# A small first load ahead of the 14-row loads in a row-sum kernel

## The chip, the cores and the metric

One core of one Trainium2 chip. The metric is the device time of one execution in microseconds (us); the profiles' spans are some 1.6 us shorter than that time and are used to say where it goes. All runs quoted are of one core.

## The reference

```python
def setup_inputs():
    batch, seq, dim = 32, 512, 1024
    return {"x": np.random.randn(batch, seq, dim).astype(np.float32), "divisor": float(dim)}

def reference(x, divisor):
    return (np.sum(x, axis=-1) / divisor).astype(np.float32)
```

16,384 rows of 1,024 float32 (67.1 MB) are read once from HBM, the chip's main memory; 64 KB are written. Each of 128 partitions has 128 rows of 4 KB to sum.

## The kernel before

All loads are issued by the SyncEngine's queue (SP), in order. Rows 0 to 119 of each partition (the main part) come in loads of 14 rows, then 8; the number beside each is how many of its rows the ScalarE (ACT) sums, while VectorE (DVE) sums the others in one instruction. The last 8 rows per partition come in ever smaller loads, so that little is left to sum when the last byte lands. Three tiles of 14 rows rotate: the fourth load waits until the first tile is summed. The first three loads wait for nothing and are put ahead of the start-up barrier.

```python
def start_loads_at_once(nc):
    first, body = nc.main_func.blocks[0], nc.main_func.blocks[1]
    loads = []
    for i in body.instructions:
        if i.engine == SP:
            if type(i).__name__ != "InstDMACopy" or (i.sync_info and i.sync_info.on_wait):
                break
            loads.append(i)
    names = {i.name for i in loads}
    ...  # moved from the body into the first block
...
    L = 8
    M = J - L                      # 120
    ...
    main = [(14, 0)] * 6 + [(14, 4), (14, 6), (8, 4)]
    last = [(4, 2), (2, 1)]
    assert sum(n for n, _ in main) == M and sum(n for n, _ in last) == L - 2
    bulk = ctx.enter_context(tc.tile_pool(name="bulk", bufs=3))
    ...
    def sums(dst, t, rows, on_act):
        d = rows - on_act
        for i in range(d, rows):
            act_sum(dst[:, i : i + 1], t[:, i, :])
        nc.vector.reduce_sum(out=dst[:, :d], in_=t[:, :d, :], axis=AX)

    j = 0
    for rows, on_act in main:
        t = bulk.tile([P, 14, D], F32, name="t")
        load(t[:, :rows, :], x_main[:, j : j + rows, :])
        sums(res[:, j : j + rows], t, rows, on_act)
        j += rows
    ...  # then loads of 4, 2 and 1 rows, and the last row in three pieces: pa, pb, pc
```

The rows of one load lie together both in HBM and in the tile, so a load is one packet per partition: 56 KB for 14 rows, 8 KB for 2. A DMA engine serves 8 partitions, 8 packets per load.

## Time and profile before

| | before |
|---|---|
| time, median of 4 runs | 161.69 us (161.69 to 161.78) |
| span of the profile | 160.1 us |
| share of the 16 DMA engines | 97.8% |
| DVE busy | 119.9 us |
| landing of the first load | 19.56 us |
| DVE's last work starts | 158.18 us |

The profile is read by the arrivals. An engine that only follows the DMA starts each instruction about 0.02 us after a load has landed, so the start times of DVE's sums in the timeline are a clock for the DMA stream. The time between two such starts for full 14-row loads is called the beat below. The prediction below shows these lines. The sum that ends the kernel, also from the timeline (start, duration, engine, line, operation):

```profile
158.18 0.49 DVE L195 TENSOR_SCALAR_CACHE_REDUCE scaled<-pc 128x322 f32<-128x322 f32 x1
```

It waits for the last piece of the last row. Whatever moves this line moves the time.

### The profile page before, as it was taken

Reading aid. Unit: us, or ns where it says so; the run is one execution under the profiler, and the core shown is the slowest. Engines: PE = TensorE matmul, PEld = TensorE weight load, DVE = VectorE, ACT = ScalarE, POOL = GpSimd, SP = SyncE. Lnnn points to the kernel's source line nnn. Section 1 sums busy time; section 2 is a strip of 40 time slices with the busy share of each in tenths; the row PEclk is TensorE's granted clock in tenths of the full one; section 3 lists DMA queues with packets and bytes.
Section 4 is the critical chain, followed back from the end, with each engine's and each line's share of the span. In section 5 each row is a group of like instructions: output and inputs, shape, how many; then the busy total and the mean of one; then the engine's idle time right before and its main releaser. Section 6 shows DMA issues by size and latency. Waiting matters only on the chain.

```text
span 160.1 us, 138 instructions
## 1 busy us (share of the span) xinstructions
DVE 119.9 (75%) x16; ACT 20.7 (13%) x39; POOL 0.8 (1%) x6
## 2 busy tenths in 40 slices
DVE  0000199968998699959995999599987990497985
ACT  3000000000000000000000000000007300491973
POOL 0000000000000000000000000000000000000010
DMA  8899999998899999998899999999799999999993
GB/s 301 387 458 458 458 458 458 458 430 358 358 458 458 458 458 458 458 458 387 358 401 458 458 458 458 458 458 430 315 401 458 458 458 458 393 393 405 415 402 104
DMA packets 2448, 67.18 MB, mean 419 GB/s; under 512 B 528, under 2 KB 912, under 8 KB 1040
## 3 DMA queue, kind: packets, MB, share of 16 engines
q1 hardware_dynamic: 2448, 67.18, 97.8%
HBM read 67.11 MB, written 0.07 MB: 419 GB/s over the span
## 4 chain that ended last, share of the span: by engine, by line
DMA 67%; DVE 29%; another core or an unknown queue 1%; SPq 1%; issue 0%; DVEq 0%
DMA t<-in_x_dram 45%; DVE res L153 28%; DMA row<-in_x_dram 22%; SPq L142 1%; DVE q L173 1%; DVE scaled L195 0%; DVE pc L190 0%; DVE fin L191 0%; DVEq L195 0%; DVEq L229 0%
## 5 line engine op out<-in xcount | busy, mean ns | idle before, releaser
L153 DVE TENSOR_REDUCE res<-t 128x14 f32<-128x14336 f32 (+3 forms) x9 | 114.4, 12716 | 37.9 <-DMA t<-in_x_dram 37.9
L147 ACT ACTIVATE junk<-t 128x1024 f32<-128x1024 f32 x17 | 17.2, 1011 | 135.2 <-DMA t<-in_x_dram 135.2
L153 DVE TENSOR_REDUCE q<-t 128x2 f32<-128x2048 f32 (+1 forms) x2 | 3.5, 1752 | 0.7 <-DMA t<-in_x_dram 0.7
L147 ACT ACTIVATION_READ_ACCUMULATOR junk<-t 128x1 f32 x17 | 3.2, 186 | 0.0
L147 ACT ACT_TABLE_LOAD x1 | 1.3, 1283 | 1.7 <-PEq L215 1.7
L186 POOL TENSOR_SCALAR res<-res 128x120 f32<-128x120 f32 x1 | 0.5, 512 | 150.5 <-DVE res L153 150.5
L173 DVE TENSOR_REDUCE q<-row 128x1 f32<-128x768 f32 x1 | 1.0, 953 | 0.1
L195 DVE TENSOR_SCALAR_CACHE_REDUCE scaled<-pc 128x322 f32<-128x322 f32 x1 | 0.5, 490 | 0.1
L147 ACT ACTIVATE junk<-pa 128x448 f32<-128x448 f32 x1 | 0.5, 547 | 0.1
L190 DVE TENSOR_REDUCE pc<-pb 128x1 f32<-128x256 f32 x1 | 0.4, 412 | 0.0
L147 ACT ACTIVATE junk<-row 128x256 f32<-128x256 f32 x1 | 0.4, 387 | 0.1
L191 DVE SCALAR_TENSOR_TENSOR fin<-q,r 128x7 f32<-128x7 f32 x1 | 0.2, 167 | 0.0
L147 ACT ACTIVATION_READ_ACCUMULATOR junk<-row 128x1 f32 x1 | 0.2, 187 | 0.0
L147 ACT ACTIVATION_READ_ACCUMULATOR junk<-pa 128x1 f32 x1 | 0.2, 186 | 0.0
L139 POOL MEMSET r<- 128x8 f32 x1 | 0.1, 104 | 1.3 <-POOLq L215 1.3
L215 POOL MEMSET const-bfloat16-1.0<- 128x1 bf16 x1 | 0.1, 101 | 0.0
L215 POOL MEMSET const-uint8-127<- 128x1 uint8 x1 | 0.1, 101 | 0.0
L215 POOL MEMSET const-float32-0.0<- 128x1 f32 x1 | 0.1, 99 | 0.2 <-issue 0.2
L215 POOL MEMSET const-float32-1.0<- 128x1 f32 x1 | 0.1, 98 | 0.0
L195 DVE DVE_READ_ACCUMULATOR scaled<-pc 128x1 f32 x1 | 0.1, 82 | 0.0
## 6 DMA issues: line engine op xcount, KB each, us to landing
t<-in_x_dram SPq DMA_DIRECT2D x8, 7168.0 KB, 35.7
t<-in_x_dram SPq DMA_DIRECT2D x1, 4096.0 KB, 28.5
t<-in_x_dram SPq DMA_DIRECT2D x1, 2048.0 KB, 33.0
t<-in_x_dram SPq DMA_DIRECT2D x1, 1024.0 KB, 35.0
row<-in_x_dram SPq DMA_DIRECT2D x1, 512.0 KB, 35.8
pa<-in_x_dram SPq DMA_DIRECT2D x1, 224.0 KB, 36.0
pc<-in_x_dram SPq DMA_DIRECT2D x1, 160.0 KB, 35.7
pb<-in_x_dram SPq DMA_DIRECT2D x1, 128.0 KB, 35.9
```

Source lines behind the costliest of these rows:

```text
L139: nc.gpsimd.memset(r, 0.0)
L142: tc.keep_in_program_order(nc.sync.dma_start(out=dst, in_=src))
L147: nc.scalar.activation(junk[:, :n], src, COPY, scale=by, accum_out=dst)
L153: nc.vector.reduce_sum(out=dst[:, :d], in_=t[:, :d, :], axis=AX)
L173: nc.vector.reduce_sum(out=q[:, j : j + 1], in_=row[:, :c], axis=AX)
L186: nc.gpsimd.tensor_scalar_mul(out=res, in0=res, scalar1=scale)
L190: nc.vector.reduce_sum(out=pc[:, D - b + 1 :], in_=pb, axis=AX)
L191: nc.vector.scalar_tensor_tensor(out=fin[:, : L - 1], in0=q[:, : L - 1], scalar=scale, in1=r[:, : L - 1], op0=MULT, op1=ADD)
L195: nc.vector.tensor_scalar(out=scaled, in0=pc, scalar1=scale, scalar2=0.0, op0=MULT, op1=ADD, accum_out=fin[:, L - 1 :])
L215: nc = _bacc.Bacc("TRN2", target_bir_lowering=False, num_devices=1)
```

## The change

Its intent: start with a load of 2 rows, whose packets are 8 KB, and take the two rows off a later load, which becomes 12.

```diff
-    main = [(14, 0)] * 6 + [(14, 4), (14, 6), (8, 4)]
+    main = [(2, 0)] + [(14, 0)] * 6 + [(14, 4), (12, 5), (8, 4)]
```

## The prediction

> **What bounds the kernel now.** I read the page first (busy shares, then the DMA lines), then the timeline for the arrival of each load, then the rate by stretches, then the DMA queue's own waits, and last the first 20 us of the DMA alone.
>
> The page, busy shares, DMA line by slices, and the queue:
>
> ```profile
> DVE 119.9 (75%) x16; ACT 20.7 (13%) x39; POOL 0.8 (1%) x6
> ...
> DMA  8899999998899999998899999999799999999993
> ...
> DMA packets 2448, 67.18 MB, mean 419 GB/s; under 512 B 528, under 2 KB 912, under 8 KB 1040
> ...
> q1 hardware_dynamic: 2448, 67.18, 97.8%
> ```
>
> The 16 DMA engines are busy for 97.8% of 160.1 us; the next busiest thing, DVE, has 25% to spare. The slices marked 7 or 8 in the middle are not holes: these views book a packet at its start, and packets here last some 2 us, so slices alternate (later ones read more than 100%). The timeline, DVE lines only, in us from the start: start, duration, and in brackets the idle time before:
>
> ```profile
> 19.58 15.09 DVE L153 TENSOR_REDUCE res<-t 128x14 f32<-128x14336 f32 x1 [19.58 <-DMA t<-in_x_dram]
> 36.52 15.09 DVE L153 TENSOR_REDUCE res<-t 128x14 f32<-128x14336 f32 x1 [1.86 <-DMA t<-in_x_dram]
> 53.47 15.09 DVE L153 TENSOR_REDUCE res<-t 128x14 f32<-128x14336 f32 x1 [1.86 <-DMA t<-in_x_dram]
> ...
> 138.18 8.69 DVE L153 TENSOR_REDUCE res<-t 128x8 f32<-128x8192 f32 x1 [6.13 <-DMA t<-in_x_dram]
> ...
> 147.89 4.42 DVE L153 TENSOR_REDUCE res<-t 128x4 f32<-128x4096 f32 x1 [1.02 <-DMA t<-in_x_dram]
> ...
> 152.79 2.29 DVE L153 TENSOR_REDUCE q<-t 128x2 f32<-128x2048 f32 x1 [0.48 <-DMA t<-in_x_dram]
> ...
> 155.29 1.22 DVE L153 TENSOR_REDUCE q<-t 128x1 f32<-128x1024 f32 x1 [0.21 <-DMA t<-in_x_dram]
> ```
>
> Every reduce of a load starts when that load lands, and DVE idles 0.2 to 6 us before it. Full loads land 16.94 to 16.95 us apart, whatever DVE does. The rate by stretches of one or two such beats (start:end, length, DVE, ACT, POOL, clock, DMA share, GB/s):
>
> ```profile
> 36.40:53.40 17.00, 15.09 (x1) 0.00 (x0) 0.00 (x0) 1.00 1.00 432
> 53.40:87.30 33.90, 30.17 (x2) 0.00 (x0) 0.00 (x0) 1.00 1.00 433
> 87.30:121.10 33.80, 30.17 (x2) 0.00 (x0) 0.00 (x0) 1.00 1.00 434
> ```
>
> The DMA share is 1.00 and the rate flat at 432 to 434 GB/s. So the time is one uninterrupted stream of 67.1 MB, plus what precedes its first byte, plus a short end. Linking packet records engine by engine, I find no pause above 0.05 us on any of the 16 engines between the first packet and the end of the loads.
>
> The DMA queue's own waits (us in total, times, longest):
>
> ```profile
> SPq L142 <- DVE res L153: 90.5, 6, 15.1
> SPq L142 <- DMA t<-in_x_dram: 25.3, 6, 17.9
> ```
>
> They look large, but they only hold back issues that are early anyway: the fourth load is issued when reduce 0 ends at 34.67, while the third load lands at 53.45, so 18.8 us of work is still queued.
>
> **What the Trainium skill says.** "DMA: Bandwidth & Descriptors", section Where 436 GB/s comes from, gives 435.2 GB/s as the limit of the 16 SBUF ports; the trace's 433 agrees within 0.5%, so there is no rate left to win. The same page, Anatomy of one DMA, gives about 2 us of fixed cost for a DMA, mostly completion, fitted on the other (GpSimd) issue path; in this queue, where the next load is already waiting, a load costs only about 0.09 us of its own (worked out below), so the fixed part shows only at the start and the end. "Perfetto Trace Analysis", section DMA Optimizations, says that splitting DMAs may let work start sooner where the DMA engines are generally idle; here they are not. The first page's Why small descriptors are slow names a fixed overhead of about 3 cycles per packet, which falls with packet size: 3 beats in 256 for 8 KB against 3 in 1792 for 56 KB, 1% of a load of 2.4 us, an estimate of 0.03 us; the trace has more, see below, and the trace decides.
>
> **The change part by part.**
>
> 1. Rows and loads. Before, the main loads are 14 x 8, then 8 rows (120); after, 2, then 14 x 7, 12, 8 (120). Same bytes, one load more, and 128 more data packets (2 rows are one 8 KB packet per partition, 8 packets per DMA engine). What a load costs beyond its bytes comes from the landings above: 14 rows take 16.945 us; 2 rows take 155.29 - 152.79 = 2.50. Slope (16.945 - 2.50)/12 = 1.204 us per row, fixed part 2.50 - 2.41 = 0.09 us. Test: 8 rows give 9.72 (measured 147.89 - 138.18 = 9.71), 4 rows 4.91 (152.79 - 147.89 = 4.90). So one more load costs 0.09 us on the path that sets the end.
>
> 2. Start. The first load landed at 19.58; less 16.945 that is a start of 2.64 us: issue, descriptor generation, the slow first packets, completion. If it stays, the landings after are: 2.64 + 2.50 = 5.14 for the 2 rows, then 22.1, 39.0, 56.0, 72.9, 89.9, 106.8, 123.75 for the fourteens, 138.3 for the twelve (14.54 us), 148.0 for the eight. Everything from there to the end is the same sequence, about 0.1 us later than before.
>
> 3. The early reduce. A reduce of 2 rows, 2.29 us, is added at 5.1, where DVE only waited before. On the late side the 12-row load gives DVE 7 rows and ACT 5 in place of 8 and 6: DVE 7.6 us (1.067 per row from 15.09 and 2.29, plus 0.15) against 8.69, ACT one row (1.01 + 0.19 us) less. DVE busy should read about 121.1, ACT about 19.5. All of it is beside the stream: after the twelve lands at 138.3, DVE is done at 145.9 and idles until 148.0. None of the gain of the earlier first reduce reaches the end, because DVE has 1.86 us of slack in every 16.95 and has nothing to catch up.
>
> 4. Buffers. Three buffers before and after, but the first now holds 2 rows. Its reduce ends at 7.4, so load 3 is issued at 7.4 rather than waiting until 34.7. Load 4 is issued at 22.1 + 15.1 = 37.2, when load 3 has until 56.0 to run; each later one 18.8 us ahead of need; the eight is issued at 121.9, 16.4 ahead. The stream is never short.
>
> 5. Semaphores. The order of instructions shows that one more load moves the rotation of DMA semaphores by one: the last small load (pc) now waits for the last fourteen (123.75) and not for the one before it (121.2). It is issued some 1.6 us later, 33 us before it lands. The early output store waits for the twelve (138.3), long before its data. No cost.
>
> 6. Slow first packets. By the packet records, each DMA engine's first 56 KB packet takes 2.25 to 3.35 us, mean about 2.9, where all later ones take 2.12; the starts are spread from 1.02 to 1.83 us and the ends from 3.85 to 4.38. The slices of the first 20 us (half a us each) show the same waves:
>
> ```profile
> DMA  0096000990029000950099009900790009500990
> GB/s 0 0 1606 229 0 0 0 573 1262 0 0 115 1720 0 0 0 1606 229 0 0 1147 688 0 0 459 1376 0 0 344 1491 0 0 0 1606 229 0 0 1376 459 0
> ```
>
> The first wave of starts falls in the third and fourth slices, the second only in the eighth and ninth. This loss of about 0.8 us per engine is the one thing on the path that the first load's shape can alter. If it is a fixed delay of the first access, it stays whatever the packet size. If it is a slower rate over the whole first packet, small packets may shorten it, and with eight of them the engines may spread less than the 0.53 us they carry to the end.
>
> Sum: +0.09 for the load, 0 for DVE, ACT, buffers and semaphores, and for the start 0 to -0.7; I take a quarter chance or so of most of it, -0.2. 161.7 + 0.09 - 0.2 = 161.6 us.
>
> **The rivals.**
>
> - The intent, a gain by early work: DVE starts at 5.1 in place of 19.6, 14.4 us sooner, and if DVE set the end the time would drop towards 150. Against it: DVE idles before every reduce for a landing. It would make nothing.
> - A shorter start: the slow first packets shrink with their size. For it, the excess in the first packet only; against it, late starters lose least (the one at 1.83 us took 2.25), which looks like a common moment before which nothing flows, about 1.7 to 2.2 us, independent of size. It would give 161.0 to 161.3.
> - A hole after the small load: it lasts 2.5 us, so the second load's descriptors must be there by about 4 us. The queue's first instructions take 0.33 to 0.43 us each and the first packet began 1.02 us after its issue, so the second load could start at about 1.5. Were there a hole, it would be 0.5 to 1 us: 162.3 to 162.8.
> - A late buffer: if issues came too late the fourteen-row beat would break; with 16 us in hand I give it almost nothing.
>
> **Range and chances.** Two per cent is 3.2 us. The start, all of it, is 2.64 us, and at most 0.8 of that is open to the change; the sure cost is 0.09. Nothing I can find reaches 2% either way. The three runs before lie within 0.1 us. The range of 161.0 to 162.0 holds the full gain at the start and a small loss there. Chances: faster 0.01, within 0.98, slower 0.01.
>
> **What would show each step right or wrong.** Right: a reduce of 2 rows at about 5.1 us; fourteens landing 16.95 apart from 22.1; the eight at 148.0; stretches still at 1.00 and 433 GB/s; DVE busy 121.1; span 160.0 to 160.3. If the small load lands well before 4.6 or the second before 21.6, the start got shorter (step 6). If the second lands after 22.5, there is a hole or the 8 KB packets are dearer than 0.09 in all (steps 1 and 2). If the beat of 16.95 changes, the address pattern matters to the rate, and my sum is void. If the first landings shift and the end does not, something behind the loads, not the stream, sets the end.

## The result, and the profile after

| | before | after |
|---|---|---|
| time, median of 4 runs | 161.69 us (161.69 to 161.78) | 161.44 us (161.41 to 161.48) |
| span | 160.1 us | 159.9 us |
| DVE busy | 119.9 us | 121.1 us |
| ACT busy | 20.7 us | 19.7 us |

The ratio is 0.9983, with a 95% interval of 0.9966 to 1.0000. Ratios here are the mean time of one kernel's fast runs over that of the other's of the same rounds, so not quite the ratio of the medians. In absolute terms 0.25 us are gone. The interval reaches 1, so this pair alone does not yet show a gain; the experiments below have to.

The page of the changed kernel, busy shares and DMA queue:

```profile
DVE 121.1 (76%) x17; ACT 19.7 (12%) x37; POOL 0.8 (1%) x6
...
q1 hardware_dynamic: 2592, 67.18, 97.9%
```

Still one DMA stream, with 144 packets more. The timeline of the changed kernel, DVE only:

```profile
4.83 2.29 DVE L153 TENSOR_REDUCE res<-t 128x2 f32<-128x2048 f32 x1 [4.83 <-DMA t<-in_x_dram]
21.76 15.09 DVE L153 TENSOR_REDUCE res<-t 128x14 f32<-128x14336 f32 x1 [14.65 <-DMA t<-in_x_dram]
38.70 15.09 DVE L153 TENSOR_REDUCE res<-t 128x14 f32<-128x14336 f32 x1 [1.85 <-DMA t<-in_x_dram]
...
137.94 7.62 DVE L153 TENSOR_REDUCE res<-t 128x7 f32<-128x7168 f32 x1 [3.72 <-DMA t<-in_x_dram]
...
147.66 4.42 DVE L153 TENSOR_REDUCE res<-t 128x4 f32<-128x4096 f32 x1 [2.09 <-DMA t<-in_x_dram]
...
157.93 0.49 DVE L195 TENSOR_SCALAR_CACHE_REDUCE scaled<-pc 128x322 f32<-128x322 f32 x1
```

DVE is at work at 4.83 in place of 19.58, and then idles 14.65 us for the next landing: the early start is given straight back. The 14-row beat is the same, 38.70 - 21.76 = 16.94. By the rates by stretches it is the same stream too:

```profile
22.00:38.90 16.90, 15.04 (x2) 0.00 (x0) 0.00 (x0) 1.00 1.00 434
38.90:72.80 33.90, 30.18 (x3) 0.00 (x0) 0.00 (x0) 1.00 1.00 433
```

The difference is at the beginning. Before, DVE began the first 14 rows at 19.58; at 16.945 us for a full load that is a start of 2.63 us. After, it began the first 2 rows at 4.83; at the 2.50 us that a 2-row load takes within the stream, a start of 2.33. So the stream started 0.30 us sooner. The load of 8 rows is then 0.23 sooner (147.66 against 147.89) and the last sum 0.25 (157.93 against 158.18): by this reckoning 0.05 to 0.07 us of the start are spent on the load added. These two numbers are the whole result.

The queue's waits are as harmless as before; there is one more of each kind:

```profile
SPq L142 <- DVE res L153: 92.8, 7, 15.1
SPq L142 <- DMA t<-in_x_dram: 24.8, 7, 14.3
```

### The profile page after: what moved, and what is told of

Read it like the earlier page. It is cut to its first block, busy times and chain, and to the rows that moved or that the text cites. A ratio compares the mean times of both kernels' runs of the same rounds, so it can differ in the third digit from the quotient of the medians.

```text
span 159.9 us, 139 instructions
## 1 busy us (share of the span) xinstructions
DVE 121.1 (76%) x17; ACT 19.7 (12%) x37; POOL 0.8 (1%) x6
## 4 chain that ended last, share of the span: by engine, by line
DMA 77%; DVE 22%; SPq 1%; issue 0%; DVEq 0%
DMA t<-in_x_dram 56%; DMA row<-in_x_dram 21%; DVE res L153 20%; SPq L142 1%; DVE q L173 1%; DVE scaled L195 0%; DVE pc L190 0%; DVE fin L191 0%; DVEq L195 0%; DVEq L229 0%
## 5 line engine op out<-in xcount | busy, mean ns | idle before, releaser
L153 DVE TENSOR_REDUCE res<-t 128x14 f32<-128x14336 f32 (+4 forms) x10 | 115.7, 11566 | 36.4 <-DMA t<-in_x_dram 36.4
L147 ACT ACTIVATE junk<-t 128x1024 f32<-128x1024 f32 x16 | 16.2, 1014 | 136.0 <-DMA t<-in_x_dram 136.0
```

The lines of the kernel that those rows point to most:

```text
L147: nc.scalar.activation(junk[:, :n], src, COPY, scale=by, accum_out=dst)
```

## The experiments

The sizes at stake are 0.1 to 0.3 us, and a chip's runs of the same kernel can scatter by as much, so each experiment is read twice: by the ratio of times, and by the start of the stream in its profile. The start is the time at which DVE begins its first sum, less what the first load takes within the stream (0.0925 + 1.204 us per row, from the prediction's step 1). The kernels of a call share a chip and the runs of the kernel before.

| kernel | first load, packets | DVE starts | start of the stream | last sum starts | median, before | ratio (95%) |
|---|---|---|---|---|---|---|
| before | 14 rows, 56 KB | 19.58 | 2.63 | 158.18 | | |
| before_again | 14 rows, 56 KB | 19.48 | 2.53 | 158.05 | 161.82, 161.74 | 1.0005 (0.9992 to 1.0017) |
| second2 | 14 rows, 56 KB | 19.38 | 2.43 | 158.02 | 161.91, 161.80 | 1.0001 (0.9986 to 1.0016) |
| early1_14 | 14 rows, 56 KB | 19.64 | 2.69 | 158.23 | 161.80, 161.74 | 1.0008 (0.9996 to 1.0021) |
| pad2 | 14 rows, 56 KB | 19.70 | 2.75 | 158.32 | 161.78, 161.71 | 1.0003 (0.9991 to 1.0015) |
| pad0 | 14 rows, 8 KB | 20.07 | 2.75 | 158.31 | 161.84, 161.71 | 1.0008 (0.9995 to 1.0021) |
| first7 | 7 rows, 28 KB | 11.02 | 2.50 | 158.09 | 161.56, 161.80 | 0.9983 (0.9970 to 0.9995) |
| first4 | 4 rows, 16 KB | 7.28 | 2.37 | 157.99 | 161.62, 161.80 | 0.9984 (0.9971 to 0.9996) |
| after | 2 rows, 8 KB | 4.83 | 2.33 | 157.93 | 161.44, 161.69 | 0.9983 (0.9966 to 1.0000) |
| after_again | 2 rows, 8 KB | 4.85 | 2.35 | 158.69 | 161.54, 161.71 | 0.9994 (0.9979 to 1.0009) |
| near2 | 2 rows, 8 KB | 4.83 | 2.33 | 157.93 | 161.52, 161.71 | 0.9992 (0.9980 to 1.0004) |
| early1_2 | 2 rows, 8 KB | 4.78 | 2.28 | 157.86 | 161.38, 161.74 | 0.9983 (0.9970 to 0.9997) |
| half2 | 2 rows, 4 KB | 4.86 | 2.30 | 157.99 | 161.65, 161.74 | 0.9992 (0.9980 to 1.0005) |
| first1 | 1 row, 4 KB | 4.01 | 2.71 | 158.28 | 161.59, 161.80 | 0.9982 (0.9969 to 0.9995) |

For pad0 its own load time is taken off, 17.32 us, and for half2 0.06 more than for 2 rows (8 packets of 7 ns). The start column is one execution each. Over the five kernels that begin with 14 rows in 56 KB packets it is 2.61 in the mean (2.43 to 2.75), over the four with 2 rows in 8 KB packets 2.32 (2.28 to 2.35): 0.29 us, and the two ranges don't touch.

The ranges are those of the profiled runs, and a profile can fall on a good run of its kernel or a bad one: second2's fell on its fastest (161.55, median 161.91), first1's on its slowest. In twelve of the fourteen profiles the time of the profiled run is its start plus 159.04 to 159.14 us (half2 159.21, after_again 159.86, see there). So, in the profiles, what makes one run slower than another is mostly its start, and single starts of the two kinds of kernel can overlap; the means differ.

From the start to the last sum it is 155.52 to 155.55 in before, before_again and early1_14, and 155.57 to 155.62 in seven kernels with one load more (second2, first1, first4, first7, after, near2, early1_2). So the load added costs about 0.05 us, whether it stands first or second. (Half2 has more packets besides, and after_again was held up on the way.)

The packet records give a second reading of the start, which needs neither DVE nor the landing: when each of the 16 DMA engines ends its share of the first load, less what these packets take later in the stream. The mean of the 16 engines is 1.90 to 2.03 us in the five kernels with 14 rows in 56 KB packets, 1.91 in pad0, 1.88 with 7 rows, 1.75 with 4, 1.66 to 1.73 in the five with 2 rows, and 1.86 in first1. The engines end about as far apart as before (0.52 us between the first and the last in the kernel before, 0.49 in the changed one). By this measure the first engine moved from 1.72 to 1.42 and the last from 2.24 to 1.91: both by about 0.3.

The theories at the outset. **A:** the very first packets are slow, and lose less when they are small; what the change gains is there. **B:** the gain comes from the later part, the 14, 12, 8 split or the shifted rotation.

### The same loads with the small one second (second2)

```diff
-    main = [(2, 0)] + [(14, 0)] * 6 + [(14, 4), (12, 5), (8, 4)]
+    main = [(14, 0), (2, 0)] + [(14, 0)] * 5 + [(14, 4), (12, 5), (8, 4)]
```

> The same loads as in the changed kernel, but the 2-row load stands second, behind a 14-row one. Theory A (what gains is that the very first packets are small; one more load costs about 0.09 us): first load lands at 19.56 as before, everything later 0.09 late, time 161.78. Rival B (the gain comes from the other part of the change, the split of the late rows into 14, 12, 8, or from the shifted rotation, or from the rows' addresses): time 161.45 like the changed kernel. Rival C (a load more costs nothing and the start alone moved): 161.69.

Median 161.91 against 161.80, ratio 1.0001: no gain. Its start was the best of the 14-row kernels, 2.43, and it still was not faster. So the order counts, and B falls: this kernel has the late 12-row load, the extra load and the shifted rotation, and lacks only the small first load. The interval is too wide to measure the cost of the extra load by the time, and too wide to settle B by itself. Its timeline does: from the start to the last sum it takes 158.02 - 2.43 = 155.59 us, 0.04 more than the kernel before (155.55), so nothing behind the start became faster.

```profile
158.02 0.49 DVE L195 TENSOR_SCALAR_CACHE_REDUCE scaled<-pc 128x322 f32<-128x322 f32 x1
```

### First loads of 1, 4 and 7 rows (first1, first4, first7)

```diff
+    main = [(1, 0)] + [(14, 0)] * 6 + [(14, 4), (13, 5), (8, 4)]     # first1
+    main = [(4, 0)] + [(14, 0)] * 6 + [(14, 4), (10, 4), (8, 4)]     # first4
+    main = [(7, 0)] + [(14, 0)] * 6 + [(14, 4), (7, 3), (8, 4)]      # first7
```

> First load of 1 row (4 KB packets), a later one of 13. Theory A1 (the time lost at the start grows with the bytes of the first packet): start a little shorter still than with 2 rows, first landing near 3.5 us, second at 20.5 or a little earlier, time 161.40 to 161.45. Rival A2 (the loss is a shared slow period up to about 2.2 us after which all run at full rate, so that only the spread between engines can change): time as with 2 rows or worse, 161.45 to 161.6. If 4 KB packets run dry before the second load's descriptors are there, 161.7 or more.

> First load of 4 rows (16 KB packets), a later one of 10. A1 (loss grows with the first packet's bytes; 0.33 us gained of 56 to 8 KB, so 0.27 gained here, less 0.09 for the load): 161.5. A2 (only small packets end inside the slow period; 16 KB at 0.6 us may still): between 161.45 and 161.7.

> First load of 7 rows (28 KB packets), a later one of 7. A1: half of the bytes, so 0.19 gained at the start less 0.09 for the load: 161.59. A2: 28 KB outlast the slow period (1.06 us of packet at full rate on top of a start at 1.0 to 1.8), so no gain: 161.78.

All three are faster than the kernel before, with intervals that exclude 1, and by the time they can't be told apart (0.9982 to 0.9984). By the start there is a grade from 7 rows (2.50) over 4 (2.37) to 2 (2.33), as A has it: a loss that grows with the first packet. It ends there. One row was expected to start a little sooner still, and its profile shows 2.71. That profile fell on its slowest run (161.80; the other five took 161.42 to 161.65), so it says that a small first load doesn't always start well, not that 1 row is worse. In the packet records one engine is a straggler there: the 16 engines end the first load 0.81 us apart, in place of 0.35 to 0.70 in the others. First7 was expected to gain little or nothing and gained 0.24 us in the medians, more than its start accounts for (0.1 us less than the mean of the 14-row starts; its profile fell on one of its two slowest runs, 161.62). A2, the fixed slow period, predicted no gain for it and let only the spread between the engines change. It is the worse fit: the engines' mean moved, from 1.98 us before to 1.68 after, and their spread hardly did. One profile does not settle a difference of 0.1 for first7.

### The changed kernel again (after_again)

> The changed kernel again, on the chip of the three that follow: 161.44.

Median 161.54 against 161.71 on that chip, but scattered, 161.26 to 162.21. The profile is of the slowest run, and shows what such a run is. DVE in its timeline:

```profile
72.67 15.09 DVE L153 TENSOR_REDUCE res<-t 128x14 f32<-128x14336 f32 x1 [1.92 <-DMA t<-in_x_dram]
89.86 15.09 DVE L153 TENSOR_REDUCE res<-t 128x14 f32<-128x14336 f32 x1 [2.10 <-DMA t<-in_x_dram]
106.97 15.09 DVE L153 TENSOR_REDUCE res<-t 128x14 f32<-128x14336 f32 x1 [2.02 <-DMA t<-in_x_dram]
124.17 10.82 DVE L153 TENSOR_REDUCE res<-t 128x10 f32<-128x10240 f32 x1 [2.11 <-DMA t<-in_x_dram]
```

The beat is 17.1 to 17.2 us here in place of 16.94, for three loads; the start (2.35) is like the other's. The stream was held up in the middle, 0.68 us in sum, by something that no other profile shows. That is the scatter against which 0.25 us has to be seen.

### The first load as long as before, in 8 KB packets (pad0, and pad2 as its control)

```diff
-        t = bulk.tile([P, 14, D], F32, name="t")
-        load(t[:, :rows, :], x_main[:, j : j + rows, :])
+        t = bulk.tile([P, 7 * (2 * D + 16)], F32, name="t")
+        if n == 0:                                  # pad2: n == 2
+            pairs = t.rearrange("p (a b) -> p a b", a=7)[:, :, : 2 * D]
+            load(pairs, x_main[:, j : j + rows, :].rearrange("p (a b) d -> p a (b d)", b=2))
+            ...  # the same 14 sums, read around the gaps; other loads as before
```

> No load more and none shorter: the first load keeps its 14 rows, but a gap of 64 bytes after every 2 rows in its tile cuts it into 8 KB packets, 56 per DMA engine instead of 8. Packet records before: 8 KB take 309 ns against 302 for a seventh of a 56 KB one, so 56 of them cost 0.37 us more. Theory A (small first packets shorten the start by 0.33): first landing at 19.6, time 161.7, and 0.33 less than the kernel with the same gap in the third load. Rival D (what gains is that the first load is short as a whole, not its packets): first landing 19.9, time 162.06, equal to that of the third load.

> The same gaps in the third load: the price of 8 KB packets without a change at the start. A and D: first landing 19.56, third load 0.37 longer (17.3 us), time 162.06. If small packets are cheaper inside the stream than I took them, nearer to 161.7; the difference from the kernel with the gap in the first load is what counts.

Pad2, DVE in its timeline:

```profile
36.59 15.09 DVE L153 TENSOR_REDUCE res<-t 128x14 f32<-128x14336 f32 x1 [1.80 <-DMA t<-in_x_dram]
53.91 15.09 DVE L162 TENSOR_REDUCE res<-t 128x14 f32<-128x14336 f32 x1 [2.23 <-DMA t<-in_x_dram]
```

The load with gaps took 53.91 - 36.59 = 17.32 us, 0.38 more than 16.94: the price of 48 small packets more per engine was as expected. The times were not: 161.78 and 161.84 in place of 162.06, because other loads ran faster in both: three of the other 14-row beats took 16.87 to 16.89 us in place of 16.94 (0.19 in sum with the rest), and from the landing of the 8-row load to the last sum it was 10.10 us, against 10.29 before. The gaps had moved the tiles of the end by 1,344 bytes, and the packets there took less (309 ns in place of 314 in the mean for 8 KB, in the packet records). But the end packets of after_again took 309 as well, without any gap, and its end took 10.28 us. So neither the place nor the packets' time is the reason, and this side effect stays unexplained.

What counts is pad0 against pad2. A expected 0.33 us in pad0's favour; it was 0.06 slower, and its start is 2.75, like pad2's. (In the packet records its engines end the first load 0.09 us sooner than pad2's in the mean and 0.15 at the last engine, beyond the price of the packets. That is at most half of what A asks for, and DVE saw none of it.) So A as I stated it falls: small packets alone do not shorten the start by 0.33. The rival that fits is D, the short first load as a whole. But a mended A fits as well: a load of 56 packets per engine has seven times the descriptors (the orders to an engine, taken here as one for each packet) to be made, and that may cost what the small packets gain. The first 5 us in slices of an eighth of a us show something of it. First the changed kernel, then pad0:

```profile
DMA  0000000099363466998999969799799999990000
GB/s 0 0 0 0 0 0 0 0 328 393 66 131 131 131 197 262 459 393 328 393 459 393 524 262 524 328 393 590 328 459 459 721 2491 1376 2753 459 0 0 0 0
```

```profile
DMA  0000000099949407137779396996969969499793
GB/s 0 0 0 0 0 0 0 0 262 393 262 66 197 66 0 131 66 131 328 262 328 459 131 721 262 459 524 262 590 262 524 524 262 655 197 459 524 328 655 131
```

Both begin at 1.0 us with the first packet of each engine, and both then starve: packets are mostly begun at 60 to 260 GB/s where 433 is the full rate. The changed kernel is at the full rate from slice 16 on, at 2.0 us; pad0 only from slice 21, at about 2.6. With 56 KB packets this period can't be seen, because it lies inside the first packet of each engine. (Rates above 433 are only packets booked at their starts.)

### Where the first rows lie in HBM (near2)

```diff
-    L = 8
+    L = 10                      # x_last now has 10 rows per partition, 40 KB apart
-    main = [(2, 0)] + [(14, 0)] * 6 + [(14, 4), (12, 5), (8, 4)]
+    main = [(14, 0)] * 6 + [(14, 4), (12, 5), (8, 4)]
+    load(t[:, :2, :], x_last[:, :2, :])             # first of all loads
```

> As the changed kernel, but the first 2 rows per partition come from a region where the partitions' rows lie 40 KB apart instead of 480 KB. If the slow start is a matter of where the first packets of the 16 engines lie in HBM (rival E), the first landing moves from 4.80 by 0.1 us or more, and the time with it. If it is only the packet size (A), first landing 4.8, time 161.44 within 0.05.

DVE started at 4.83, to the digit as in the changed kernel; 161.52 against 161.54 for the changed kernel. A pitch of 40 KB in place of about 480 between the partitions changes nothing: E falls, as far as this change of address tests it.

### The kernel before against itself (before_again)

> The kernel before against itself: how far two starts of the same kernel lie apart. Three profiles with a 14-row load first had it land at 19.56, 19.35 and 19.68 us; four with small first loads were 0.2 to 0.4 sooner for their bytes. Expected: first landing 19.35 to 19.7, ratio 1.000 within 0.001. If it lands at 19.2 or sooner, the gain of the changed kernel at the start is not told from chance.

Start 2.53, ratio 1.0005. As expected; the scatter of the start with 14 rows is about 0.3 us from best to worst.

### Only the first load ahead of the barrier (early1_14, early1_2)

```diff
+    loads = loads[:1]
     names = {i.name for i in loads}
```

> The kernel before, but only the first load is issued ahead of the start-up barrier; loads 2 and 3 follow it at about 1.7 us instead of at 0.43 and 0.88. Theory F (the first packets are slow because the descriptors of the second and third load are being made meanwhile): first landing 0.2 to 0.5 sooner, 19.1 to 19.3, time about 161.4. Theory A (the slow start comes of the size of the first packets): unchanged, 19.35 to 19.7, 161.7. In both the second load is there long before it is needed.

> The changed kernel with only the first, 2-row load ahead of the barrier; the others are issued at about 1.7 us and could move from about 2.7, the first load ends at about 4.2. Theory F: first landing 4.5 or sooner and the end sooner as well, 161.2. Theory A: first landing 4.8, the same time as the changed kernel. If the second load's descriptors come late there is a hole: second landing over 21.9 and the time up by as much.

Neither start moved: 2.69 with 14 rows, 2.28 with 2. That speaks against F, but the test came out weaker than I had planned. The second load was not issued at 1.7 us: the barrier waits for SP, and with one load ahead of it in place of three SP reaches it sooner. ACT's first instruction starts at 0.78 us here, against 1.74 in the kernel before. SP's queue in the timeline of early1_14, of a window from 0.4 to 0.8 us:

```profile
0.79 0.33 SPq L143 DMA_DIRECT2D t<-in_x_dram  x1
```

So the second load was moved by 0.36 us only (from 0.43), the third by 0.26 (from 0.91 to 1.17). Had the making of their descriptors held up the first load, some of that should have shown in the start, and none did; a longer delay was not tried. Early1_2 has the lowest median of all, 161.38, but its ratio of 0.9983 is that of the changed kernel in its first call. It is not shown to be better.

### The small load in 4 KB packets (half2)

```diff
+        if j == 0:
+            t = bulk.tile([P, 14 * D], F32, name="t")
+            t = t[:, : rows * (D + 16)].rearrange("p (r d) -> p r d", r=rows)[:, :, :D]
+        else:
+            t = bulk.tile([P, 14, D], F32, name="t")
```

> The changed kernel, but a gap of 64 bytes between the two rows in the first tile cuts the 8 KB packets into two of 4 KB: 16 per DMA engine in place of 8, the load as short as before. Theory A (small packets start better): first landing 4.8 to 4.9 (8 more packets at 7 ns are 0.06). Theory G (each packet's descriptor of the first load takes time at the start, which is what the 56 packets of the 14-row load with gaps paid): 4.9 to 5.2, as 48 more packets there cost about 0.3 to 0.5 us of start, 8 more some 0.05 to 0.1. Time as the changed kernel plus the same.

DVE started at 4.86, 0.01 to 0.08 after the four 2-row kernels of 8 KB packets. Eight more packets per engine at 7 ns are 0.06. So 16 descriptors per engine cost nothing visible beyond their packets, and half the packet size gains nothing either. G is neither shown nor refuted: it expected 0.05 to 0.1 on top, at the edge of what one profile can tell. The time, 161.65, ratio 0.9992, is between.

### What they say together

Without a small first load the five ratios are 1.0001 to 1.0008; with one (1, 2, 4 or 7 rows, after included) the eight are 0.9982 to 0.9994. No single interval is narrow enough, but the two groups don't overlap, on either chip on which both kinds were run. The ratios of a call share their runs of the kernel before, so they are not independent. Taken together by call, all runs without a small first load (the kernel before included) against all with one, the means are 161.85 against 161.58, 161.76 against 161.60 and 161.79 against 161.54 us: 0.16 to 0.27 sooner, over 57 runs and 37. Shown: the gain needs the short load to be first; it is a start of the stream 0.29 us sooner; the partitions' pitch in HBM and the later split have no part in it. Not shown: why. Packet size alone, as large as A had it, is refuted by pad0; whether the load's length counts by itself, or small packets count and many descriptors take the gain back, is open. A kernel with two 28 KB packets per partition, and one with the second load held back by 2 us or more, would be the next to run.

## Why the prediction was right

The time, 161.44, lies in the range of 161.0 to 162.0, and the middle of 161.6 was 0.16 too high. The range would have held no change at all as well (161.69), so what tests the mechanism is the landings.

- **The bound** held: share 1.00 at 433 to 434 GB/s, a beat of 16.94, and DVE's early start given back as 14.65 us of idle time.
- **Step 1, the load added:** put at 0.09, it measured about 0.05 (from the start to the last sum 155.59 us in the mean of the seven kernels with a load more, 155.54 in three without). The predicted 0.09 came from loads at the end of the stream, where packets of 8 KB take 314 ns in the mean. In second2, where the added load runs inside the stream, they take 309; for 8 packets that is 0.04 less, which fits.
- **Step 2 and 6, the start:** this term was mis-sized. I booked -0.2 as a chance of a larger gain; it was -0.30 in this pair and -0.29 over nine profiles. DVE began the small load at 4.83 rather than 5.14. That the engines might spread less did not come true (0.49 us against 0.52); their mean moved. The argument that I set against it, that late starters lose least and so a common moment must pass, is only half true: there is a starved period up to about 2.0 us, but 28 KB, 16 KB and 8 KB first packets came out of it with less lost than 56 KB.
- **What to look for:** I had said that a landing well before 4.6, or a second one before 21.6, would show a shorter start. Both limits were too strict: with DVE beginning them at 4.83 and 21.76 the start was already 0.3 shorter. Of the signs of being right, three were missed on the same account: the fourteens from 22.1 (21.76), the eight at 148.0 (147.66) and a span of 160.0 to 160.3 (159.9).
- **Step 3:** DVE busy 121.1 as predicted, ACT 19.7 (19.5 predicted), 7.62 us for the 7 rows.
- **A reading:** the 19.58 that the prediction calls a landing is DVE's start; the load landed at 19.56. It changes nothing, as the sums use starts throughout. Not all later 56 KB packets took 2.12 us: one engine's second took 2.38.
- **Steps 4 and 5:** no load came late. The last small load was issued at 124.45, 2.3 us later than before and not 1.6, as the whole row of small issues waits for the tile of the 8-row load; it is still 33 us ahead of its landing.
- **The rivals:** the gain by early work made nothing, as said; no hole followed the small load (second landing 21.76, a full beat and no more after 4.83); the shorter start was the one that came true, though with 161.44 short of the 161.0 to 161.3 that I gave it.

## What to carry to other kernels

When a queue of DMAs sets the time, read it by its landings: what precedes the first byte, the beat, the end. Making an idle engine begin sooner is worth nothing unless it has a backlog. A short first load started the stream 0.3 us sooner here at a price of 0.05, so it is worth a try in a kernel tuned to the last us; but check by moving the small load to second place that it is the start that pays.

## What the Trainium skill lacked or had wrong

- "DMA: Bandwidth & Descriptors", section Where 436 GB/s comes from, says that for transfers between HBM and SBUF (the core's on-chip memory) the HBM side, about 358 GB/s, binds. With one core at work it did not: 432 to 434 GB/s over whole beats, at the 435 that the page gives for the SBUF ports. The page's section Measured does limit the 358 to two cores of a pair streaming at once; the sentence lacks that condition.
- The same page, section Measured, gives 6.15 us (341 GB/s) for 1 MB. That is for a DMA on another issue path; in this queue a load of 1.05 MB took 2.50 us (419 GB/s), and one load more cost about 0.05 us. The page has no figure for a load that is queued behind another.
- No page has the slow start that follows the first packets: they begin at 1.0 us after the first issue, the engines then starve until about 2.0 us (2.6 with 56 packets per engine in the first load), and the start of the stream is 2.32 us with a 2-row first load against 2.61 with 14 rows.
